# One product for the first 64 queries of a sliding-window attention block, with the low parts of the probabilities in the unused half of the rows

## The chip, the cores and the metric

The kernel runs on one core of one Trainium2 chip. The metric is the device time of one execution, in microseconds (us). A core has the engines TensorE (PE; weight loads are shown as PEld), VectorE (DVE), ScalarE (ACT), GpSimd (POOL) and SyncE (SP, which here only issues transfers), an SBUF of 128 partitions, and PSUM for the results of products.

## The reference

One transformer layer on 512 tokens of width 2048: RMS norm, sliding-window attention with a learned bias and sinks, a gate, an output projection, then a gated embedding and a final norm. Cut to what matters here (32 heads of 64 in 4 key-value heads; blocks of 128 queries):

```python
q, k, v, gate = jnp.split(h @ w_in, [...], axis=-1)
dist = qi + BLOCK - kj
band = (dist >= 0) & (dist < WINDOW)          # WINDOW = 128
scores = einsum('bnqhgd,bnjhd->bnhgqj', q, kb) * HEAD_DIM ** -0.5 + bias
scores = where(mask, scores, finfo.min)
m = maximum(scores.max(-1), sink)
e = exp(scores - m)
probs = e / (e.sum(-1) + exp(sink - m))
out = einsum('bnhgqj,bnjhd->bnqhgd', probs, vb)
y = (out * silu(gate)) @ w_out
```

A query sees its own key and the 127 before it. The first 64 queries therefore see at most 64 keys.

## The kernel before

All products keep float32 accuracy with operands that are split in two: a rounded high part (type fp32r) and a low part, the remainder. A weight product is three products, high by high, high by low and low by high (`mm3`, L123).

**Stages.** The first stage (loop over 16 slabs k, L199) computes keys, values and the first two chunks of queries while it loads x. The second (L850 to L915) runs everything else of the attention: the remaining query chunks and all gate chunks as a stream of products (`projections`, L829), and between them 64 attention blocks. The third and fourth are the output projection and the gated embedding, both as Strassen-like schemes whose combined weights are summed in DRAM during the second stage (`sum_weights`, L663): SP copies a block of weights (L666), and GpSimd adds another to the copy with an accumulating transfer (L668), which must wait for the copy to land. Copies and additions are spread over the blocks; eight copies are issued in the first one (`SUMS_EARLY`).

**An attention block.** Block i belongs to a quad of heads d = i // 8 and to 64 queries g = i % 8 (`UNITS` is 8, `TWOS` is 8). It runs through three generators in successive turns of the main loop, with the projection's products between their steps:
- `scores(i)` (L449): two products on TensorE into the one PSUM tile of the tag w; GpSimd puts the sink into a column and fills masked columns (L477, L480); VectorE adds the bias and takes the maximum (L485 to L494); ScalarE takes the exponentials with their sum (L498) and writes the normalised probabilities `pr` (L509).
- `turn(i)` (L511), two turns later: TensorE transposes pr (L518), so that keys lie on the partitions; ScalarE takes the high part `r[:, 0]` (L523), VectorE the low part `r[:, 1]` (L524). For g of 2 and more GpSimd cuts out a triangle, `own` (L534).
- `weigh(i)` (L546), one turn later: TensorE multiplies the values with r, high and then low part (L559, L560). The values V[t] hold, for each key-value head, 64 columns of high and 64 of low parts, so that one product gives both (L360); the two halves of the result are added on ScalarE and VectorE (L571, L573).

**Values.** At the end of the first stage VectorE scales the values of four token tiles and splits V[0] (L374 to L380, `split` at L362). The splits of V[1] to V[3] and the differences DV of neighbouring tiles are made in the first blocks (`first_chores`, L430); SP spreads the differences over partitions (L428).

**Order.** In the second stage the order on all engines is the order in which the program is written. Each engine's queue is taken in order, SP's too: a transfer that waits holds up all that SP issues after it. SP's order around the change is: the last weights of the first stage; the four transfers of the first bias (`load_bias(0)`, L851, which reads a table that GpSimd wrote to DRAM); the weight slabs of the projections (`Weights.load`, L99), each 128 x 1024 floats, in a pool of three; the first eight copies of the weight sums; a further slab; the differences DV. A slab is split by ScalarE and VectorE (`Weights._make`, L104), in order with the work of the attention blocks on these engines.

**Tiles.** Pools are stacked. `mid` holds the keys and values, then the attention's pool `attn`, which takes the room of the first stage's pool `start`. A tile whose room was used before waits for the old users.

Of the kernel before, what the change touches and what calls it, by code (L numbers as in the profile page):

```python
# [11 lines left out]
F32 = mybir.dt.float32  # L12
F32R = mybir.dt.float32r
# [7 lines left out]
P = 128  # L21
KC = D // P
NB = S // P
HEADS = 32
KVH = 4
HD = 64
# [3 lines left out]
HB = P // 2  # L30
# [8 lines left out]
MASKED = -3.0e38  # L39
# [16 lines left out]
def trunk_kernel(ctx: ExitStack, tc: tile.TileContext, a: dict):  # L56
    nc = tc.nc
# [18 lines left out]
    mid = ExitStack()  # L76
# [44 lines left out]
    W = Weights(ahead=2)  # L121
# [60 lines left out]
    kinds, g = [], 0  # L182
# [16 lines left out]
    for k in range(KC):  # L199
# [7 lines left out]
        both = start_pool.tile([P, 2, 768], F32R, tag="w0s", name=f"w0s{k}")  # L207
# [11 lines left out]
        h = room.tile([P, S], F32R, tag="ah", name=f"xh{k}")  # L219
        l = room.tile([P, S], F32R, tag="al", name=f"xl{k}")  # L220
# [36 lines left out]
        f, e = k == 0, k == KC - 1  # L257
# [26 lines left out]
        if 3 <= k < 3 + NB:  # L284
            t = k - 3
# [74 lines left out]
    V = [kvq.tile([P, KVH, 2, HD], F32R, name=f"V{t}") for t in range(NB)]  # L360
# [13 lines left out]
    for t in range(NB):  # L374
        nc.vector.tensor_scalar_mul(values[t], v_ps[t][:, :256], rstd1[:, t : t + 1])
        nc.vector.scalar_tensor_tensor(
            out=values[t], in0=v_ps[t][:, 256:], scalar=rstd1[:, t : t + 1], in1=values[t], op0=ALU.mult, op1=ALU.add
# [11 lines left out]
    for b in range(exact, BUCKETS):  # L389
        d = np.nonzero(bk == b)[0]  # L390
        if len(d):
            lo, n = P - 1 + int(d.min()), len(d)
# [4 lines left out]
    pre.close()  # L397
    banks_s.close()
    spsum = mid.enter_context(tc.tile_pool(name="psum_w", bufs=1, space=PSUM))
    apool = mid.enter_context(tc.tile_pool(name="attn", bufs=1, reuse_waits="tile"))  # L400


# [3 lines left out]

    U, T, PT, O, gates, biases = {}, {}, {}, {}, {}, {}

    DV = apool.tile([P, NB - 1, 2, KVH * 2 * HD], F32R, name="DV")
    apool.tile([P, 8], F32, name="pad2")  # L410
    diffs = {}

    def make_diff(n):
# [35 lines left out]
    def scores(i):  # L449

        d, g = divmod(i, UNITS)
        if g == 4 and d + 1 < TWOS:
            load_bias(d + 1)
        key = K[d // 2]

        s_ps = spsum.tile([P, 2, S], F32, tag="w", name=f"s{i}")  # L460
        number = [min(2 * g + u + 1, 5) * QB for u in range(2)]
        for u in range(2):
            first, n = max(2 * g + u - 4, 0) * QB, number[u]
            st = Q[d][:, 2 * g + u].rearrange("p h q -> p (h q)")
            nc.tensor.matmul(s_ps[:, u, : 2 * n], st, key[:, :, first : first + n], start=True, stop=True)  # L465
        W = KEYS + 2
        t = apool.tile([P, 2, W], F32, tag="t", name=f"t{i}", bufs=3)
        at = t[:, 0, 0:1]

        def two(of, stride, n):  # L470
            return bass.AP(tensor=at.tensor, offset=at.offset + of, ap=[at.ap[0], [stride, 2], [1, n]])

        late = QB if g >= 2 else 0
        seen = [t[:, 0, 0 : P + 1], t[:, 1, 1 + late : P + 2 + late] if late else t[:, 1, 0 : P + 1]]
        both = two(0, W + 1 + late if late else W, P + 1)
        pr = [t[:, u, 1 + late * u : 1 + late * u + P] for u in range(2)]
        nc.gpsimd.tensor_copy(two(0, W + W - 1 if late else W, 1), sinkb[:, d : d + 1].unsqueeze(1).to_broadcast([P, 2, 1]))  # L477
        for u, n in enumerate(number):
            if n < P:
                nc.gpsimd.memset(t[:, u, 1 + n : 1 + P], MASKED)  # L480
        yield
        bias = biases[d][:, ::-1]
        if g < 2:
            for u, n in enumerate(number):
                nc.vector.tensor_add(t[:, u, 1 : 1 + n], s_ps[:, u, :n], bias[:, KEYS - n :])  # L485
            for u, n in enumerate(number):
                nc.vector.tensor_add(t[:, u, 1 : 1 + n], s_ps[:, u, n : 2 * n], t[:, u, 1 : 1 + n])
        else:
            x = t[:, :, 1 : 1 + KEYS]
            nc.vector.tensor_add(x, s_ps[:, :, :KEYS], bias.unsqueeze(1).to_broadcast([P, 2, KEYS]))  # L490
            nc.vector.tensor_add(x, s_ps[:, :, KEYS : 2 * KEYS], x)
            nc.vector.tensor_max(two(1, W + P, QB), t[:, :, 1 : 1 + QB], t[:, :, 1 + P : 1 + KEYS])
        sm = apool.tile([P, 24], F32, tag="sm", name=f"sm{i}", bufs=4)
        nc.vector.tensor_reduce(sm[:, 0:2], both, axis=AX.X, op=ALU.max, negate=True)  # L494
        yield
        for u in range(2):
            su = seen[u]
            nc.scalar.activation(su, su, AF.Exp, bias=sm[:, u : u + 1], accum_out=sm[:, 2 + u : 3 + u])  # L498
        yield
        nc.vector.reciprocal(sm[:, 4:6], sm[:, 2:4])  # L500
        yield

        T[i] = apool.tile([P, 2, P], F32, tag="pr", name=f"pr{i}", bufs=3)
        for u in range(2):
            out, src = T[i][:, u], pr[u]
            if late and (g + u) % 2:
                out = out.rearrange("p (h k) -> p h k", h=2)[:, ::-1]
                src = src.rearrange("p (h k) -> p h k", h=2)
            nc.scalar.mul(out, src, sm[:, 4 + u : 5 + u])  # L509

    def turn(i):  # L511


        d, g = divmod(i, UNITS)
        pr = T.pop(i)
        pt = bank(f"pt{i}", "t")[:, :256]
        for u in range(2):
            nc.tensor.transpose(pt[:, u * P : (u + 1) * P], pr[:, u, :], ident)  # L518

        r = apool.tile([P, 2, 256], F32R, tag="r", name=f"r{i}", bufs=2)  # L520
        rh, rl = (r[:, l].rearrange("p (h u q) -> p u h q", h=4, u=2) for l in range(2))
        src = pt.rearrange("p (u h q) -> p u h q", u=2, h=4)
        nc.scalar.copy(rh, src)  # L523
        nc.vector.tensor_sub(rl, src, rh.bitcast(F32))  # L524
        yield
        own = None
        if g >= 2:
            own = apool.tile([P, 2, 256], F32R, tag="own", name=f"own{i}", bufs=2)
            rows = slice(0, P) if g % 2 else slice(0, HB)
            flat = lambda v: v[rows].rearrange("p l (u q) -> p (l u) q", q=HB)  # L530


            sign = -1 if g % 2 else 1
            nc.gpsimd.affine_select(  # L534
                out=flat(own), in_=flat(r).bitcast(F32), pattern=[[0, 8], [sign, HB]], compare_op=ALU.is_ge, fill=0.0,
                base=-HB - 1 if g % 2 else 0, channel_multiplier=-sign,
            )
        PT[i] = (r, own)
        yield
        if own is not None:  # L540
            here, there = slice(HB, P), slice(0, HB)
            if g % 2 == 0:
                here, there = there, here
            nc.scalar.copy(own[there, 0], own[here, 1].bitcast(F32))

    def weigh(i):  # L546

        d, g = divmod(i, UNITS)
        n, b = divmod(g, 2)
        kv = d // 2  # L550
        r, own = PT.pop(i)
        if g == 0:
            U[d] = apool.tile([P, 2, S], F32, tag="u", name=f"u{d}", bufs=3)
        if b == 0:
            O[d] = bank(f"o{i}", "o").rearrange("p (b u e q) -> p b u e q", b=2, u=2, e=2)
        ops = O[d]
        out = ops[:, b].rearrange("p u e q -> p (u e q)")
        first = V[0 if n == 0 else n - 1 + b][:, kv]
        for low in range(2):  # L559
            nc.tensor.matmul(out, first, r[:, low], start=low == 0, stop=own is None and low == 1)  # L560
        if own is not None:
            nc.tensor.matmul(
                out, DV[:, n - 1, b, kv * 2 * HD : (kv + 1) * 2 * HD], own[:, 0], start=False, stop=True
            )
        yield
        if b:
            dst = U[d][:, :, n * P : (n + 1) * P].rearrange("p u (b q) -> p b u q", b=2)
            lower, upper = slice(0, 64), slice(64, 128)
            tmp = [apool.tile([P, 2, 2, HB], F32, tag=f"tmp{e}", name=f"tmp{e}_{i}", bufs=1) for e in range(2)]
            for e, (o, x) in enumerate(((lower, upper), (upper, lower))):  # L570
                nc.scalar.copy(tmp[e][o], ops[x, :, :, e, :])  # L571
            for e, o in enumerate((lower, upper)):
                nc.vector.tensor_add(dst[o], ops[o, :, :, e, :], tmp[e][o])  # L573
        if g == UNITS - 1:
            for c in (2 * d, 2 * d + 1):
                weighed.add(c)
                if c in open_gates:
                    idle.append(partial_of(gate_value, c))
# [67 lines left out]
    for (nm, p), small in zip(SUMS, (7, 5, 6, 4, None, None)):  # L646
        for m in range(2 if small else 0):
            t = summed["small", small, m] = tc.dram_tile([P, WE], F32, name=f"small_{small}_{m}")
# [5 lines left out]
        for jj in range(2):  # L654
            for m in range(4):
                t = summed[nm, p, jj, m] = tc.dram_tile([P, WE], F32, name=f"{nm}_{p}_{jj}_{m}")
# [265 lines left out]
    late = pool("late", reuse_waits="tile")  # L922
# [350 lines left out]
    f = ple_forms.made[4]  # L1273
# [18 lines left out]
    two = gate(3, 1, ps, e)  # L1292
# [143 lines left out]
```

## Time and profile before

Times are of the kernel as a whole. The profiled execution is a run of its own; its span is the time between its first and last instruction.

| | us |
|---|---|
| runs | 794.17, 794.43, 794.76; median 794.43 |
| span of the profiled execution | 792.6 |
| TensorE busy | 782.8 (99% of the span) |
| VectorE busy | 600.1 (76%) |
| ScalarE busy | 507.5 (64%) |
| GpSimd busy | 123.8 (16%) |

How to read it: the share of busy time is of the whole span. The chain of waits follows the work that ended last back from the end, at each step to what released it. A view in order of time has one row per instruction or per run of equal ones: start, duration, engine, line, operation, output and input tile, sizes, count, and in brackets how long the engine sat idle before it and what ended that. Lines are those of the kernel before. Transfers are shown when they are issued ("SPq"); another view gives the time from issue to landing. q1 is SP's transfer queue and q0 GpSimd's; both are worked off by the same 16 transfer engines. Times run from the span's start.

### The profile page before, as it was taken

The page shows a single profiled execution, that of the slowest core. Times are in us where ns is not written, and L with a number is a line of the kernel's source. Part 1 is how long each engine was busy: PE and PEld are TensorE (multiplying, and loading weights), DVE is VectorE, ACT ScalarE, POOL GpSimd, SP SyncE. Part 2 cuts the span into 40 slices and gives each one's busy share as a digit, 9 for nine tenths or more (in the row PEclk, how much of TensorE's full clock was granted, in tenths as well). Part 3 has the DMA queues.
Part 4 walks back from the last instruction along what each step waited for, and adds up shares of the span by engine and source line. Part 5 has one row for each costly group of instructions (what it writes and reads, how often), then busy time and mean ns, then how long its engine had stood idle before and what let it go on. Part 6 is the DMA issues. An engine that isn't in the chain of part 4 may idle for free.

```text
span 792.6 us, 11069 instructions
## 1 busy us (share of the span) xinstructions
PE 782.8 (99%) x3746; PEld 655.7 (83%) x3746; DVE 600.1 (76%) x1043; ACT 507.5 (64%) x1066; POOL 123.8 (16%) x248
## 2 busy tenths in 40 slices
PE   9999999999999999999999999999999999999995
PEld 8888888888888888888888888888888888888885
DVE  4556697877878687877777899778866757988896
ACT  6742576666767586766666654466699656656765
POOL 0201413131212213122222200000000120210000
PEclk9999999999999999999999999999999999999998
DMA  8987999797989989898987498667864996787633
GB/s 337 300 215 259 211 272 302 213 277 205 280 226 263 236 246 253 233 249 233 242 230 183 137 366 326 209 209 227 282 240 142 345 204 197 159 229 217 180 107 106
DMA packets 45065, 185.22 MB, mean 234 GB/s; under 512 B 6656, under 2 KB 7680, under 8 KB 39888
## 3 DMA queue, kind: packets, MB, share of 16 engines
q1 hardware_dynamic: 36928, 143.30, 53.3%
q0 software_dynamic: 8080, 41.22, 27.1%
q8 instruction: 29, 0.48, 0.2%
q14 instruction: 28, 0.23, 0.1%
HBM read 177.63 MB, written 62.97 MB: 304 GB/s over the span
## 4 chain that ended last, share of the span: by engine, by line
PE 99%; DVE 0%; ACT 0%; ACTq 0%; issue 0%; DVEq 0%
PE gps L128 7%; PE gps L127 7%; PE gps L126 7%; PE qps L126 7%; PE qps L128 7%; PE qps L127 7%; PE g L128 6%; PE o L127 6%; PE g L126 6%; PE o L128 6%; PE o L126 5%; PE g L127 5%; PE s L465 2%; PE o L560 2%; PE vps L279 2%; PE pt L518 2%
## 5 line engine op out<-in xcount | busy, mean ns | idle before, releaser
L705 DVE TENSOR_TENSOR blo<-braw,bhi 128x1024 fp32r<-128x1024 f32 x102 | 124.3, 1221 | 41.6 <-ACT bhi L704 41.3
L704 ACT CAST bhi<-braw 128x1024 fp32r<-128x1024 f32 x102 | 107.3, 1052 | 73.6 <-PE o L128 24.9
L128 PE MATMUL gps<-xh,wlo 128*128 128x512 f32 x256 | 99.9, 390 | 0.0
L127 PE MATMUL gps<-xl,whi 128*128 128x512 f32 x256 | 99.8, 390 | 0.0
L126 PE MATMUL gps<-xh,whi 128*128 128x512 f32 x256 | 99.8, 390 | 0.0
L126 PE MATMUL qps<-xh,whi 128*128 128x512 f32 x224 | 87.7, 391 | 0.0
L128 PE MATMUL qps<-xh,wlo 128*128 128x512 f32 x224 | 87.5, 390 | 0.0
L127 PE MATMUL qps<-xl,whi 128*128 128x512 f32 x224 | 87.3, 390 | 0.0
L126 PE MATMUL g<-bhi,fhg 128*128 128x512 f32 x192 | 75.1, 391 | 0.0
L110 DVE TENSOR_TENSOR wlo<-wraw,whi 128x1024 fp32r<-128x1024 f32 x60 | 73.5, 1226 | 1.9 <-ACT whi L109 1.5
L126 PE MATMUL o<-bhi,fho 128*128 128x512 f32 x192 | 74.8, 390 | 0.0
L128 PE MATMUL g<-bhi,flg 128*128 128x512 f32 x192 | 74.8, 389 | 0.0
L128 PE MATMUL o<-bhi,flo 128*128 128x512 f32 x192 | 74.8, 389 | 0.0
L127 PE MATMUL g<-blo,fhg 128*128 128x512 f32 x192 | 74.7, 389 | 0.0
L127 PE MATMUL o<-blo,fho 128*128 128x512 f32 x192 | 74.7, 389 | 0.0
L534 POOL TENSOR_SCALAR_AFFINE_SELECT own<-r 64x512 fp32r<-64x512 f32 (+1 forms) x48 | 32.4, 675 | 249.0 <-DVE r L524 241.5
L524 DVE TENSOR_TENSOR r<-pt,r 128x256 fp32r<-128x256 f32 x64 | 27.1, 423 | 55.4 <-ACT r L523 54.6
L523 ACT CAST r<-pt 128x256 fp32r<-128x256 f32 x64 | 23.7, 371 | 70.6 <-PE pt L518 70.2
L109 ACT CAST whi<-wraw 128x1024 fp32r<-128x1024 f32 x60 | 62.3, 1040 | 4.6 <-issue 4.1
L128 PEld LDWEIGHTS gps<-xh,wlo 128*128 128x128 f32 x256 | 48.0, 188 | 10.1
L498 ACT ACTIVATE t<-t,sm 128x129 f32<-128x129 f32 x128 | 50.6, 397 | 8.5 <-DVE sm L494 7.0
L126 PEld LDWEIGHTS gps<-xh,whi 128*128 128x128 f32 x256 | 48.1, 188 | 9.0
(228 smaller groups left out, 1741.3 us busy)
## 6 DMA issues: line engine op xcount, KB each, us to landing
wraw<-in_w_gate_in SPq DMA_DIRECT2D x32, 512.0 KB, 7.1
w_out<-in_w_out POOLq DMA_DIRECT2D x32, 512.0 KB, 8.0
braw<-w_out SPq DMA_DIRECT2D x32, 512.0 KB, 4.8
wraw<-in_w_q SPq DMA_DIRECT2D x28, 512.0 KB, 5.2
braw<-in_ple_gate SPq DMA_DIRECT2D x24, 512.0 KB, 4.3
braw<-in_w_out SPq DMA_DIRECT2D x22, 512.0 KB, 4.3
xw<-in_first SPq DMA_DIRECT2D x14, 640.5 KB, 7.1
w_out<-in_w_out SPq DMA_DIRECT2D x16, 512.0 KB, 10.1
```

The lines of the kernel that those rows point to most:

```text
L109: nc.scalar.copy(hi, raw)
L110: nc.vector.tensor_sub(lo, raw, hi.bitcast(F32))
L126: nc.tensor.matmul(ps, sh, mh, start=first, stop=False, skip_group_check=more)
L127: nc.tensor.matmul(ps, sh, ml, start=False, stop=False, skip_group_check=more)
L128: nc.tensor.matmul(ps, sl, mh, start=False, stop=last, skip_group_check=more)
L279: nc.tensor.matmul(v_ps[t], h[:, c], both[:, :, 256:512], start=f, stop=e, skip_group_check=True)
L498: nc.scalar.activation(su, su, AF.Exp, bias=sm[:, u : u + 1], accum_out=sm[:, 2 + u : 3 + u])
L523: nc.scalar.copy(rh, src)
L524: nc.vector.tensor_sub(rl, src, rh.bitcast(F32))
L534: nc.gpsimd.affine_select(out=flat(own), in_=flat(r).bitcast(F32), pattern=[[0, 8], [sign, HB]], compare_op=ALU.is_ge, fill=0.0, base=-HB ...
L704: nc.scalar.copy(hi, raw)
L705: nc.vector.tensor_sub(lo, raw, hi.bitcast(F32))
```

## The change

For g = 0, the first 64 queries of each quad of heads, only 64 keys exist. The changed kernel writes the normalised probabilities of these 64 keys twice, side by side, so that after the transpose both halves of the partitions hold them. ScalarE takes the high part of all 128 rows into `r[:, 0]`, and VectorE overwrites the upper 64 rows with the low part. A new tile `twice` holds the first 64 rows of V[0] in both halves of its partitions; two transfers on SP's queue fill it, right after the pools of the attention are opened. One product of `twice` with `r[:, 0]` takes the place of the two products of V[0] with high and low part. The scores' tile is filled, reduced and exponentiated over 64 columns and the sink where it was 128 and the sink. DV, pr, r and own move with `twice` into a pool of their own, `operands`, ahead of `attn`; a padding tile of 8 floats goes.

```diff
+    operands = mid.enter_context(tc.tile_pool(name="operands", bufs=1, reuse_waits="tile"))
     apool = mid.enter_context(tc.tile_pool(name="attn", bufs=1, reuse_waits="tile"))
...
-    DV = apool.tile([P, NB - 1, 2, KVH * 2 * HD], F32R, name="DV")
-    apool.tile([P, 8], F32, name="pad2")
+    DV = operands.tile([P, NB - 1, 2, KVH * 2 * HD], F32R, name="DV")
+    twice = operands.tile([P, KVH * 2 * HD], F32R, name="twice")
+    for o in range(2):
+        src = V[0][:HB].rearrange("p h l d -> p (h l d)").bitcast(F32)
+        nc.sync.dma_start(twice[HB * o : HB * o + HB].bitcast(F32), src)
...
+        near = P if g else HB
+        if g == 0:
+            seen = [v[:, : near + 1] for v in seen]
+        both = two(0, W + 1 + late if late else W, near + 1)
+        pr = [t[:, u, 1 + late * u : 1 + late * u + near] for u in range(2)]
...
-            if n < P:
-                nc.gpsimd.memset(t[:, u, 1 + n : 1 + P], MASKED)
+            if n < near:
+                nc.gpsimd.memset(t[:, u, 1 + n : 1 + near], MASKED)
...
+            if g == 0:
+                out, src = out.rearrange("p (h k) -> p h k", h=2), src.unsqueeze(1).to_broadcast([P, 2, HB])
...
         nc.scalar.copy(rh, src)
-        nc.vector.tensor_sub(rl, src, rh.bitcast(F32))
+        if g == 0:
+            nc.vector.tensor_sub(rh[HB:], src[HB:], rh[HB:].bitcast(F32))
+        else:
+            nc.vector.tensor_sub(rl, src, rh.bitcast(F32))
...
-        for low in range(2):
+        if g == 0:
+            nc.tensor.matmul(out, twice[:, kv * 2 * HD : (kv + 1) * 2 * HD], r[:, 0], start=True, stop=True)
+        for low in range(2 if g else 0):
             nc.tensor.matmul(out, first, r[:, low], start=low == 0, stop=own is None and low == 1)
```

More of the change, by code (lines that the diff above doesn't have):

```diff
@@ L474, in scores @@
         seen = [t[:, 0, 0 : P + 1], t[:, 1, 1 + late : P + 2 + late] if late else t[:, 1, 0 : P + 1]]
-        both = two(0, W + 1 + late if late else W, P + 1)
-        pr = [t[:, u, 1 + late * u : 1 + late * u + P] for u in range(2)]
+        near = P if g else HB
[3 more added lines that the diff above has]
+        pr = [t[:, u, 1 + late * u : 1 + late * u + near] for u in range(2)]
         nc.gpsimd.tensor_copy(two(0, W + W - 1 if late else W, 1), sinkb[:, d : d + 1].unsqueeze(1).to_broadcast([P, 2, 1]))
         for u, n in enumerate(number):
-            if n < P:
-                nc.gpsimd.memset(t[:, u, 1 + n : 1 + P], MASKED)
+            if n < near:
+                nc.gpsimd.memset(t[:, u, 1 + n : 1 + near], MASKED)
         yield
@@ L501, in scores @@
         yield
-        T[i] = apool.tile([P, 2, P], F32, tag="pr", name=f"pr{i}", bufs=3)
+        T[i] = operands.tile([P, 2, P], F32, tag="pr", name=f"pr{i}", bufs=3)
         for u in range(2):
             out, src = T[i][:, u], pr[u]
+            if g == 0:
+                out, src = out.rearrange("p (h k) -> p h k", h=2), src.unsqueeze(1).to_broadcast([P, 2, HB])
             if late and (g + u) % 2:
@@ L518, in turn @@
             nc.tensor.transpose(pt[:, u * P : (u + 1) * P], pr[:, u, :], ident)
-        r = apool.tile([P, 2, 256], F32R, tag="r", name=f"r{i}", bufs=2)
+        r = operands.tile([P, 2, 256], F32R, tag="r", name=f"r{i}", bufs=2)
         rh, rl = (r[:, l].rearrange("p (h u q) -> p u h q", h=4, u=2) for l in range(2))
@@ L527, in turn @@
         if g >= 2:
-            own = apool.tile([P, 2, 256], F32R, tag="own", name=f"own{i}", bufs=2)
+            own = operands.tile([P, 2, 256], F32R, tag="own", name=f"own{i}", bufs=2)
             rows = slice(0, P) if g % 2 else slice(0, HB)
```

## The prediction

> **What bounds the kernel now.** I read the page first, for the busy shares and the chain that ended last.
>
> ```profile
> PE 782.8 (99%) x3746; PEld 655.7 (83%) x3746; DVE 600.1 (76%) x1043; ACT 507.5 (64%) x1066; POOL 123.8 (16%) x248
> PE 99%; DVE 0%; ACT 0%; ACTq 0%; issue 0%; DVEq 0%
> ```
>
> TensorE is busy 99% of the span and is itself the chain. So a product taken away is worth its own spacing, a microsecond by which TensorE has to wait is a microsecond of the kernel, and work on the other engines is free until TensorE waits for it. The change adds two transfers to SP's queue, so the second view is the order of time of that queue between the first stage (keys, values, first queries) and the attention, with VectorE's beside it. Columns: start, duration, engine, line, operation, count.
>
> ```profile
> 63.02 1.72 SPq L447 DMA_DIRECT2D bias<-tdram  x4
> 64.84 0.84 SPq L102 DMA_DIRECT2D wraw<-in_w_q  x2
> 65.73 1.23 SPq L666 DMA_DIRECT2D small<-in_w_out  x2
> 67.01 4.35 SPq L666 DMA_DIRECT2D w_out<-in_w_out  x6
> 81.28 0.35 SPq L102 DMA_DIRECT2D wraw<-in_w_gate_in  x1
> 89.12 2.42 SPq L428 DMA_DIRECT2D DV<-diffs  x4
> 91.59 0.58 SPq L102 DMA_DIRECT2D wraw<-in_w_gate_in  x1
> ...
> 79.16 0.41 DVE L365 TENSOR_TENSOR V<-values,V 128x256 fp32r<-128x256 f32 x1
> ```
>
> From 63.0 to 71.4 us SP issues the first bias, two weight slabs (call them W4 and W5, counting the loads of L102 from 0) and eight copies of 512 KB (c1 to c8) that begin the weight sums. W6 follows at 81.28, W7 at 91.59. The low half of V[0] is finished only at 79.16 + 0.41 = 79.57.
>
> **The change part by part.** *Removed.* One of two 256-column products in each of the eight g = 0 blocks. The spacing of such products, from a run of four near the end (first and last), and in place:
>
> ```profile
> 782.52 0.28 PE L127 MATMUL last<-low,fhg 128*128 128x256 f32 x1
> ...
> 782.88 0.28 PE L127 MATMUL e<-blo,pTh 128*128 128x256 f32 x1
> ...
> 97.42 0.48 PE L560 MATMUL o<-r,V 128*128 128x256 f32 x2
> 97.73 0.46 PE L465 MATMUL s<-k,q 128*128 128x320 f32 x2
> ```
>
> (782.88 - 782.52) / 3 = 0.12 us; in place (97.73 - 97.42) / 2 = 0.155. I take 0.14: 8 x 0.14 = 1.1 us gained (1.0 to 1.2). That is below 0.2% of the time, 1.6 us, which is about what a measurement of this kernel can tell from no change.
>
> *Shortened, at nothing.* Exponentials over 65 columns for 129, a shorter maximum, eight fill operations fewer on POOL, and a subtraction of the same width on half the partitions: all on engines at 76% and less. The new product waits for that subtraction as the second one did before. The moved tiles change no order on any engine in the built program.
>
> *Added.* Two transfers of 128 KB into `twice`, ahead of the first bias on SP's queue, and they wait for V[0]. SP issues in order, so everything behind them waits too: the bias, W4, W5, c1 to c8, W6. The DV transfers have the same shape, and four take 2.42 us, so two take 1.2: the bias goes out at 79.57 + 1.2 = 80.8 for 63.02, a shift of 17.8 us. It is priced by when each transfer lands. The rows are issues with their time to landing in us, from narrow windows: the fourth bias (issued 64.32), W4 (64.84), W5 (65.30), c1 (65.73), c8 (70.35), W6 (81.28), W7 (91.59), then POOL's accumulations a1 (81.80) and a5 (88.09).
>
> ```profile
> bias<-tdram SPq DMA_DIRECT2D x1, 20.0 KB, 2.0
> wraw<-in_w_q SPq DMA_DIRECT2D x1, 512.0 KB, 4.0
> wraw<-in_w_q SPq DMA_DIRECT2D x1, 512.0 KB, 5.0
> small<-in_w_out SPq DMA_DIRECT2D x1, 512.0 KB, 7.8
> w_out<-in_w_out SPq DMA_DIRECT2D x1, 512.0 KB, 13.4
> wraw<-in_w_gate_in SPq DMA_DIRECT2D x1, 512.0 KB, 4.3
> wraw<-in_w_gate_in SPq DMA_DIRECT2D x1, 512.0 KB, 12.0
> ...
> small<-in_w_out POOLq DMA_DIRECT2D x1, 512.0 KB, 7.1
> w_out<-in_w_out POOLq DMA_DIRECT2D x1, 512.0 KB, 12.3
> ```
>
> Bias: 66.3 becomes 84.1, while the second block's scores (TensorE at about 87) need the first's two additions (0.7 us) done: covered. W4: 68.8 becomes 86.6. ScalarE splits it at 81.98 now, and the first probabilities, which stand behind it on ScalarE, end at 86.85 + 0.70 = 87.55, that is 5.6 us later, for a transpose at 91.97:
>
> ```profile
> 81.98 1.05 ACT L109 CAST whi<-wraw 128x1024 fp32r<-128x1024 f32 x1 [4.08 <-issue]
> ...
> 86.85 0.70 ACT L509 ACTIVATE pr<-t,sm 128x128 f32<-128x128 f32 x2 [0.23 <-DVE sm L500]
> ...
> 91.97 0.38 PE L518 MATMUL pt<-ident,pr 128*128 128x128 f32 x2
> ```
>
> 86.6 + 5.6 = 92.2: some 0.2 us late, nearly covered. W6 is the costly one. If c1 to c8 only shift, c1 lands at 73.6 + 17.8 = 91.4 and c8 at 83.8 + 17.8 = 101.6. But POOL's a1 may start once c1 has landed, so the accumulations, which today run after the copies, now run among them. What that does is seen where POOL's queue (q0) and SP's (q1, the DV transfers) overlap today, from 94 to 97 us (packets, MB, share of the 16 engines; the third row is q0 from 83.0 to 84.2, its first packets there):
>
> ```profile
> q0 software_dynamic: 85, 0.57, 93.0%
> q1 hardware_dynamic: 84, 0.14, 14.2%
> ...
> q0 software_dynamic: 2, 0.02, 11.2%
> ```
>
> They take turns packet by packet, 85 to 84, and one of POOL's holds an engine 0.93 x 16 x 3 / 85 = 0.53 us by this row; alone, a1 to a5 land from 88.9 to 100.4, with the DV transfers among the last of them, so I take 0.6 for each of the four packets that an engine has of an accumulation (512 KB in packets of 0.57 MB / 85, 6.7 KB on the mean with small closing ones among them, over 16 engines). A copy is one packet on each engine, (101.6 - 91.4) / 7 = 1.46 us; a weight slab has 128 rows of 4 KB, eight on each engine, and W4 and W5 land 1.5 us apart, 0.18 a packet. Today a1's first packets run just before 84.2, about 2.3 us after its issue at 81.80; issued at about 91.4 it starts at 93.7. From there c8 lacks 7.9 us, 5.4 turns, each made longer by 0.6: 101.6 + 3.2 = 104.8. W6's eight packets then take 8 x (0.18 + 0.6) = 6.2: W6 lands at 111.0. Its bounds: 101.6 + 1.5 = 103.1 if q1 goes first, and 103.1 + 5 x 2.4 = 115.1 if all five accumulations do.
>
> Who waits for W6 is in ScalarE's order of time: the split of W6 and, behind it, pr of block 3; the split of W7 and pr of block 4; and TensorE's transposes of them.
>
> ```profile
> 99.29 1.05 ACT L109 CAST whi<-wraw 128x1024 fp32r<-128x1024 f32 x1
> ...
> 103.90 0.69 ACT L509 ACTIVATE pr<-t,sm 128x128 f32<-128x128 f32 x2 [0.30 <-DVE sm L500]
> ...
> 104.80 1.04 ACT L109 CAST whi<-wraw 128x1024 fp32r<-128x1024 f32 x1
> ...
> 109.14 0.69 ACT L509 ACTIVATE pr<-t,sm 128x128 f32<-128x128 f32 x2
> ...
> 108.35 0.27 PE L518 MATMUL pt<-ident,pr 128*128 128x128 f32 x1
> ...
> 114.00 0.27 PE L518 MATMUL pt<-ident,pr 128*128 128x128 f32 x1
> ```
>
> From split to pr's end it is 5.3 us (VectorE's low part, a query split and the reciprocal lie between), and the transpose comes at 108.35, so W6 may land until 108.35 - 5.3 - 0.2 = 102.8 without a wait. At 111.0 TensorE waits 8.2 us there (0.3 to 12.3). W7 is not an addition to it but a second check of the same delay: behind W6 stand the DV transfers (16 packets, 1.6 us alone) and W7 (1.5), with 20 - 5.4 - 8 = 6.6 accumulation packets left (4.0): 111.0 + 7.1 = 118.1. It may land until 114.00 - 5.0 - 0.2 = 108.8: 9.3 late in all. The later slabs come as far behind W7 as today, so TensorE, 9 us late itself, then meets them.
>
> A wait of 8 us has one more price. At the end of the kernel and at its start the trace shows what idleness does to TensorE's granted clock (columns of the windows: stretch and length, busy of PE, PEld, DVE, ACT, POOL, clock, DMA share, GB/s).
>
> ```profile
> 783.40:786.00 2.60, 0.24 (x3) 0.04 (x1) 2.31 (x10) 2.29 (x4) 0.00 (x0) 1.00 0.00 0
> 786.00:787.40 1.40, 0.00 (x0) 0.00 (x0) 1.26 (x5) 1.14 (x4) 0.00 (x0) 0.99 0.00 0
> 787.40:790.00 2.60, 0.00 (x0) 0.00 (x0) 0.33 (x1) 0.37 (x1) 0.00 (x0) 0.50 0.92 295
> ...
> 4.17 1.22 PE L265 MATMUL qps<-xh,w0s 128*128 128x256 f32 x4
> ...
> 5.61 0.70 PE L265 MATMUL qps<-xh,w0s 128*128 128x256 f32 x4
> ```
>
> The clock halves 787.4 - 783.6 = 3.8 us after the last product, and at the start four products of 256 columns take 1.22 us at 4.17 and 0.70 from 5.61 on, so TensorE has come to its full pace by about 5.6. So after an 8 us gap TensorE may run at half speed for up to some 5 us: 0 to 2.5 lost, I take 2. [...]
>
> *Sum.* Wait at block 3's transpose 8.2 + half clock 2.0 = 10.2, which covers W7's 9.3; less 1.1: +9.1 us. Against the profiled execution's span of 792.6 that is 801.7; what lies around the span, 794.43 - 792.6 = 1.8, is taken as unchanged: **803.5 us**.
>
> **The rivals.** (a) *Hidden after all, not slower.* W6 lands at 103.1 because SP's copies keep their 1.46 us beside the accumulations, 0.3 us late; then W7 is in time (103.1 + 1.6 + 1.5 = 106.2, under 108.8) and the products decide: 794.43 + 0.3 - 1.1 = 793.6. For it: W6 has 13.7 us to spare today (85.6 to 99.29). Against: the shift is 17.8, and the 85-to-84 row. It decides up to a landing at 103.9, where the wait eats the 1.1 gained. (b) *Partly hidden.* The accumulations start later or cost less among copies, W6 lands around 106: 3.2 us of wait, too short for the clock, and W7 around 113, 4 us late: 794.43 + 4.2 - 1.1 = 797.5. For it: 0.53 us per packet in the row, not 0.6. (c) *Turns by whole transfers.* A queue is served a whole transfer's packets before the other: a copy (1.46) per accumulation (2.4) from 93.7, so 5.4 x 2.4 = 13.0, of which there are only 12: c8 at 113.6, W6 at 115.1, 12.3 of wait plus 2: 794.43 + 14.3 - 1.1 = 807.6. Against: both kinds in the row have four packets per engine and transfer, so it doesn't exclude this, but equal counts over only 3 us speak for single turns. [...] (d) *A real gain*, above 1.6 us, would need TensorE to wait for softmax work today; the chain shows 99% TensorE.
>
> **How the numbers follow.** Forecast 0.66, (b) 0.13, (c) 0.08, (a) 0.10, (d) 0.03. The likeliest case alone, with the clock's 0 to 2.5 and W6 at 109 to 113, spans 800 to 806. Holding 8 in 10 means taking in (b) and (c): 796.5 to 808.0. Slower than 0.2%: 0.66 + 0.13 + 0.08 = 0.87; within it 0.10; faster 0.03.
>
> **What would show it.** In the changed profile: SP's bias transfers issued at 80 to 81 us; W6 landing at 109 to 113; ScalarE idle before its split for a DMA; one TensorE gap of about 8 us ahead of block 3's transpose, near 108 us, followed by lower granted clock; the eight lone products of the g = 0 blocks; and from some 130 us on the old rhythm of 5.65 us a block. Wrong would be: no TensorE gap, or gaps that recur in every pair, or W6 in before 103 us.

## The result, and the profile after

| | before | changed |
|---|---|---|
| median of the runs | 794.43 us (794.09 to 795.12) | 808.85 us (808.54 to 810.0) |
| span of the profiled execution | 792.6 us | 808.3 us |
| TensorE busy | 782.8 us (99%) | 787.1 us (97%) |

The change makes the kernel slower: ratio 1.0184, 95% interval 1.0173 to 1.0195, or 14.4 us between the medians. The prediction had 803.5 us and a range to 808.0. The profiled execution of the changed kernel took 810.0 us, 1.2 us above its median, so a sum over its trace should come out near 15.6.

The page of the changed kernel: its busy times, the chain that ended last, TensorE and its granted clock in 40 slices of 20 us, and the rows of the groups that show a new idle time.

```profile
PE 787.1 (97%) x3738; PEld 657.6 (81%) x3738; DVE 600.0 (74%) x1043; ACT 506.6 (63%) x1066; POOL 124.4 (15%) x240
...
PE   9999959999999999999999999999999999999995
...
PEclk9999989999999999999999999999999999999998
...
PE 91%; DMA 4%; DVE 2%; ACT 1%; SPq 1%; issue 0%; ACTq 0%; DVEq 0%
...
L109 ACT CAST whi<-wraw 128x1024 fp32r<-128x1024 f32 x60 | 62.3, 1041 | 25.1 <-DMA wraw<-in_w_gate_in 15.1
```

Eight products and eight fills are gone (3738 for 3746, 240 for 248), and yet TensorE is busy 4.3 us longer: part of its work ran at a lower clock. The chain now has 4% of transfers and 1% of SP's queue. TensorE's idle time is in the sixth slice, 101 to 121 us, with the lower clock. The waits of TensorE (engine and line, what it waited for: us in total, times, longest) show that it is two gaps there, one forecast and one not:

```profile
PE gps L126 <- DVE q L321: 8.2, 1, 8.2
PE o L576 <- ACT own L556: 3.0, 2, 2.8
...
PE pt L527 <- ACT pr L518: 0.4, 1, 0.4
```

The row left out, 0.9 us at the very start, is the only one that the kernel before has too (0.8). SP's queue in order of time, at the place where the prediction read it:

```profile
80.12 1.17 SPq L414 DMA_DIRECT2D twice<-V  x2
81.39 1.93 SPq L451 DMA_DIRECT2D bias<-tdram  x4
83.35 0.90 SPq L102 DMA_DIRECT2D wraw<-in_w_q  x2
84.30 1.20 SPq L680 DMA_DIRECT2D small<-in_w_out  x2
85.54 4.06 SPq L680 DMA_DIRECT2D w_out<-in_w_out  x6
90.71 0.34 SPq L102 DMA_DIRECT2D wraw<-in_w_gate_in  x1
...
101.04 0.33 SPq L102 DMA_DIRECT2D wraw<-in_w_gate_in  x1
```

The bias goes out at 81.39 instead of 63.02, and everything behind it moves with it; W6 goes out at 90.71 and W7 at 101.04, both 9.4 us later than before. Their issue is not what costs. These are the times from issue to landing of W4 (issued 83.35), c8 (89.11), W6 and W7, each from a narrow window of the changed kernel:

```profile
wraw<-in_w_q SPq DMA_DIRECT2D x1, 512.0 KB, 4.5
...
w_out<-in_w_out SPq DMA_DIRECT2D x1, 512.0 KB, 16.6
...
wraw<-in_w_gate_in SPq DMA_DIRECT2D x1, 512.0 KB, 21.1
...
wraw<-in_w_gate_in SPq DMA_DIRECT2D x1, 512.0 KB, 19.7
```

So c8 lands at 105.7, W6 at 111.8 and W7 at 120.7, the slabs 26.2 and 17.1 us later than before (85.6 and 103.6). ScalarE in order of time shows who stands behind the two slabs in the changed kernel:

```profile
111.80 1.04 ACT L109 CAST whi<-wraw 128x1024 fp32r<-128x1024 f32 x1 [10.22 <-DMA wraw<-in_w_gate_in]
...
120.79 1.04 ACT L109 CAST whi<-wraw 128x1024 fp32r<-128x1024 f32 x1 [3.39 <-DMA wraw<-in_w_gate_in]
121.86 0.74 ACT L585 COPY tmp<-o 64x256 f32<-64x256 f32 x2
122.51 0.40 ACT L556 CAST own<-own 64x256 fp32r<-64x256 f32 x1
```

VectorE's part between W6's split and the products:

```profile
112.88 1.23 DVE L110 TENSOR_TENSOR wlo<-wraw,whi 128x1024 fp32r<-128x1024 f32 x1 [10.40 <-ACT whi L109]
114.12 1.39 DVE L321 TENSOR_TENSOR q<-qps,q 64x512 fp32r<-64x512 f32 x2
```

TensorE in order of time, the last product ahead of the first gap and the first behind each:

```profile
107.09 0.39 PE L128 MATMUL qps<-xh,wlo 128*128 128x512 f32 x1
115.66 0.76 PE L126 MATMUL gps<-xh,whi 128*128 128x512 f32 x1 [8.18 <-DVE q L321]
...
122.96 0.58 PE L576 MATMUL o<-own,DV 128*128 128x256 f32 x1 [2.82 <-ACT own L556]
```

W6 lands at 111.8; its high part (1.04), its low part (1.23) and the query split behind that (1.39), which empties the PSUM bank, follow at once, and 3.9 us after the landing the first product of the next chunk of gates starts, 8.18 us late. W7 lands at 120.7. Its split stands ahead of the copy of `own` on ScalarE, and the product with `own` starts 2.82 us late. What the clock did to the work between, in windows (stretch and length, busy of PE, PEld, DVE, ACT, POOL, granted clock, DMA share, GB/s):

```profile
107.50:112.60 5.10, 0.00 (x0) 0.00 (x0) 0.00 (x0) 0.80 (x1) 0.00 (x0) 1.00 1.04 234
112.60:119.40 6.80, 3.75 (x9) 3.00 (x10) 5.40 (x11) 2.27 (x9) 0.81 (x2) 0.50 1.01 255
119.40:122.80 3.40, 0.74 (x6) 0.44 (x4) 0.93 (x1) 1.97 (x4) 0.00 (x0) 1.00 0.53 126
122.80:126.20 3.40, 3.24 (x9) 2.75 (x10) 3.31 (x9) 2.23 (x9) 0.71 (x2) 0.50 1.05 284
```

There are two stretches at half clock, one after each gap. Work of 3.75 and of 3.24 us at 0.50 lost half of that, 1.9 and 1.6 us (the product with `own` at 122.96 took 0.58 us there; one of the same size takes 0.28 at 135.85, where the clock is 1.00). The transfer engines, by contrast, are full throughout the first gap: the slabs were late because there was that much to move ahead of them. What had been lost stands earlier in the two pages, in the row of the transfer engines' busy share over 40 slices, first before, then changed:

```profile
DMA  8987999797989989898987498667864996787633
DMA  9870999989799999989896588767782997796633
```

In the fourth slice, about 60 to 80 us, they are at seven tenths before (259 GB/s) and next to idle in the changed kernel (26 GB/s). While SP waits for V[0] hardly anything is fetched, and what was not fetched then stands ahead of W6 and W7.

### The profile page after: what moved, and what is told of

Read it like the earlier page. It is cut to its first block, busy times and chain, and to the rows that moved or that the text cites. A ratio compares the mean times of both kernels' runs of the same rounds, so it can differ in the third digit from the quotient of the medians.

```text
span 808.3 us, 11051 instructions
## 1 busy us (share of the span) xinstructions
PE 787.1 (97%) x3738; PEld 657.6 (81%) x3738; DVE 600.0 (74%) x1043; ACT 506.6 (63%) x1066; POOL 124.4 (15%) x240
## 4 chain that ended last, share of the span: by engine, by line
PE 91%; DMA 4%; DVE 2%; ACT 1%; SPq 1%; issue 0%; ACTq 0%; DVEq 0%
PE gps L126 7%; PE gps L127 7%; PE gps L128 7%; PE qps L126 6%; PE qps L128 6%; PE qps L127 6%; PE o L127 5%; PE o L128 5%; PE o L126 5%; PE g L127 5%; PE g L126 5%; PE g L128 5%; DMA wraw<-in_w_gate_in 2%; PE s L469 2%; PE vps L279 2%; DMA w_out<-in_w_out 2%
## 5 line engine op out<-in xcount | busy, mean ns | idle before, releaser
L110 DVE TENSOR_TENSOR wlo<-wraw,whi 128x1024 fp32r<-128x1024 f32 x60 | 73.5, 1227 | 21.2 <-ACT whi L109 21.1
L127 PEld LDWEIGHTS gps<-xl,whi 128*128 128x128 f32 x256 | 48.8, 191 | 9.1
L505 ACT ACTIVATE t<-t,sm 128x129 f32<-128x129 f32 (+1 forms) x128 | 49.7, 390 | 7.8 <-DVE sm L501 6.3
```

The source lines that it names most:

```text
L110: nc.vector.tensor_sub(lo, raw, hi.bitcast(F32))
L127: nc.tensor.matmul(ps, sh, ml, start=False, stop=False, skip_group_check=more)
```

## The experiments

The theory after this result: the two transfers hold SP's queue until V[0] is split, so the eight early copies, GpSimd's accumulations and the weight slabs meet in one heap; the loss is the wait for W6 and a second one at W7, each with its half clock, and the new arithmetic is a small gain. The rivals: the arithmetic itself costs, or the moved tiles; the late bias costs; the copies alone cost, without the accumulations.

**The transfers without the arithmetic, and the arithmetic without the early transfers.** The first kernel is the one before with only the transfers added; the second is the changed kernel with the transfers behind the eight copies.

```diff
     DV = apool.tile([P, NB - 1, 2, KVH * 2 * HD], F32R, name="DV")
-    apool.tile([P, 8], F32, name="pad2")
+    twice = apool.tile([P, KVH * 2 * HD], F32R, name="twice")
+    for o in range(2):
+        src = V[0][:HB].rearrange("p h l d -> p (h l d)").bitcast(F32)
+        nc.sync.dma_start(twice[HB * o : HB * o + HB].bitcast(F32), src)
```

> The kernel before with only the two transfers added in the place where the change puts them (and the padding tile left out for room); nothing reads the tile twice, and the two products stay. Queue theory: the loss is there without any of the new arithmetic, and without its gain: 808.85 + 0.6 to 1.1, so 809 to 811, with the gap of about 8 us before the products of W6 and one of about 3 us before those of own. Rival (arithmetic or tiles): 794 to 796.

```diff
-    for o in range(2):
+
+    def load_twice():
         src = V[0][:HB].rearrange("p h l d -> p (h l d)").bitcast(F32)
-        nc.sync.dma_start(twice[HB * o : HB * o + HB].bitcast(F32), src)
+        for o in range(2):
+            nc.sync.dma_start(twice[HB * o : HB * o + HB].bitcast(F32), src)
...
             for n in sums_in(i):
                 sum_weights(n)
+        if i == 0:
+            load_twice()
```

> The changed kernel with the two transfers into twice moved behind the eight early copies on SP's queue, nothing else. Queue theory (the whole loss is the queue that stands behind the two transfers while they wait for V[0]): the bias is issued at 63 us again and c1 to c8 from 66 on, the transfers at 79.6 to 80.8, W6 still at about 81.3; no wait of TensorE, no low clock, and only the saved products count: 793.3 to 793.9 (the blocks after the stall gained 0.08 us each in the changed kernel's trace, 0.6 in all; 1.1 by the prediction). Rival (the new product itself, the wait for its operands or the moved tiles cost): still 800 or more.

The transfers alone took 811.61 us, ratio 1.021 (1.0196 to 1.0224), 0.6 us above the expected range, with the same two waits of TensorE, both somewhat longer:

```profile
PE gps L126 <- DVE q L321: 8.8, 1, 8.8
PE o L565 <- ACT own L547: 4.0, 2, 2.3
```

The changed kernel with late transfers took 793.41 us, ratio 0.999 (0.9981 to 0.9999). TensorE's only wait is the 0.8 us at the start again, and SP's queue has its old order, with W4, W5 and the eight copies right behind the bias:

```profile
59.86 1.72 SPq L454 DMA_DIRECT2D bias<-tdram  x4
...
80.00 1.14 SPq L416 DMA_DIRECT2D twice<-V  x2
81.63 0.34 SPq L102 DMA_DIRECT2D wraw<-in_w_gate_in  x1
```

The two transfers still wait for V[0] until 80.0, but nothing urgent stands behind them now. All of the loss is their place in the queue; arithmetic and moved tiles are not to blame. This version is faster than both kernels, than the one before by 0.1%, only just clear of the noise.

**What the two transfers cost where they stand in nobody's way.** The kernel before, with the transfers at that late place.

```diff
-    apool.tile([P, 8], F32, name="pad2")
+    twice = apool.tile([P, KVH * 2 * HD], F32R, name="twice")
+
+    def load_twice():
...
+        if i == 0:
+            load_twice()
```

> The kernel before with the two transfers added behind the eight early copies (and without the padding tile); the two products stay and nothing reads twice. Queue theory: they cost nothing there, 794.2 to 795.0; and the step to the same place with the new product, 793.41, is then the product's. Rival (the transfers cost or the tiles gain): 793.4, or 796 and more.

Measured: 794.29 us against 794.36, ratio 1.0000 (0.9991 to 1.0008). They cost nothing there. Beside the run before, 793.41, that leaves 0.9 us for the new arithmetic: 0.11 per product taken away (the interval of that run alone allows 0.1 to 1.5 us). The traces are sharper than the times: from the first product with r to the scores behind it are 0.31 us before (97.42 to 97.73) and 0.20 in the late version (97.78 to 97.98), and in each of the eight g = 0 blocks, there and in the changed kernel, this stretch is 0.12 us shorter, 0.9 in all.

**The bias ahead of the transfers.** The four transfers of the first bias keep their time; the slabs and copies stay behind the transfers into `twice`.

```diff
...
     load_bias(0)
+    load_twice()
     W.apart = True
```

> The changed kernel with the first bias ahead of the two transfers, everything behind them as in the changed kernel. Queue theory by way of W6 and W7: the bias counts for nothing, the loss stays: 808 to 810 (W4 goes out 1.8 us earlier, and so do the copies: at best 807). Rival (the late bias holds up the first softmax and so the rest): back to 794 to 796.

Measured: 808.15 us, ratio 1.0166 (1.015 to 1.0181), waits of 7.3 and 2.6 us at the same two places. The late bias is not the cause.

**The changed kernel without the first five accumulations.**

```diff
-        elif i % 2 == 1 and 0 <= i // 2 - 3 < len(adds):
+        elif i % 2 == 1 and 5 <= i // 2 - 3 < len(adds):
             nc.gpsimd.dma_start(*adds[i // 2 - 3], accum_op=ALU.add, max_dma_last_dim=8192)
```

> The changed kernel without GpSimd's first five accumulating transfers (a1 to a5; that part of the weight sums is left out, everything else is done). If the accumulations' turns make W6 and W7 late: c1 to c8 land from 90.6 at 1.46 us each, c8 at 101, W6 at about 103 and W7 at about 106, in time for both waits: no wait but the 0.4 us at block 0's transpose, 793.5 to 795.5. If the copies alone suffice: gaps remain, 800 or more.

Measured: 798.37 us, ratio 1.0052 (1.0039 to 1.0066). The waits of TensorE, then ScalarE's split of W6:

```profile
PE o L576 <- ACT own L556: 2.1, 2, 1.1
PE gps L126 <- DVE q L321: 1.6, 1, 1.6
```

```profile
104.76 1.05 ACT L109 CAST whi<-wraw 128x1024 fp32r<-128x1024 f32 x1 [3.69 <-DMA wraw<-in_w_gate_in]
```

Some 10 of the 14 us go with the five accumulations: W6 is there at 104.8 instead of 111.8. But the expectation was missed by 3 us. The shift alone, without any accumulation, is already too much, by 1.6 us of wait for W6 and 2.1 at the products with `own`: c8 lands at 101.2, as expected, but W6 only 3.5 us behind it, where some 2 were put. The clock stays at full behind these waits, 1.00 from 105 to 143 us.

**The copies ahead of the transfers, the slabs behind.**

```diff
...
     proj = projections()
+    for n in range(0, SUMS_EARLY, 2):
+        sum_weights(n)
+    load_twice()
     load_bias(0)
...
         if i == 0:
-            return range(0, SUMS_EARLY, 2)
+            return range(0)
```

> The changed kernel with the eight early copies issued ahead of the two transfers; the transfers, the first bias, W4 and W5 stay in the order of the changed kernel, so they are as late as there. If copies and accumulations in front of W6 and W7 make the loss: W6 lands before 90 us, at most some tenths of a us of wait from W4 at block 0's transpose, 793.3 to 795. If the late bias, W4 and W5 make it: no better than 805.

Measured: 801.45 us, ratio 1.0088 (1.0074 to 1.0102): between what the theories had. W6, expected before 90 us, landed at 99.3. TensorE's longest wait lies elsewhere, and W4, issued at 82.95, took 10.1 us to land:

```profile
PE pt L530 <- ACT pr L521: 4.9, 1, 4.9
```

```profile
wraw<-in_w_q SPq DMA_DIRECT2D x1, 512.0 KB, 10.1
```

With the copies long landed, GpSimd's accumulations go out at 81.9, beside the slabs and no longer beside the copies. Now W4 is late (93.1; the transposes of the first probabilities stand behind its split). It is the same cause at another slab: loaded beside the accumulations, it takes 2.5 times its 4.0 us of before.

**The second wait, taken away where it showed.** The split of W7 is put behind the attention work of its turn on ScalarE, so that the copy of `own` does not wait for it.

```diff
             if n == 0:
                 first_chores(i, 1)
-                some(W.todo)
+                if i != 4:
+                    some(W.todo)
...
             elif n == 5:
                 next(softmax, None)
+                if i == 4:
+                    some(W.todo)
```

> The changed kernel with one step moved: in block 4's turn of the loop the split of W7 stands behind that turn's attention work on ScalarE and VectorE (the copies out of o, the copy within own, the exponentials), not ahead of it. If the second wait of the changed kernel is own's copy standing behind W7's split, as its trace reads: the first gap of 8.2 us stays, the wait of 2.8 us of the product with own goes, and with it part of the half clock: 803.5 to 806. If TensorE would wait for W7 itself as long: 808 to 809.5. (W8's load moves behind the last DV transfers, which may cost 1 to 2 us later.)

Measured: 811.58 us, ratio 1.0215 (1.02 to 1.0231), against expectation. The wait for `own` behind W7 is gone, but the next one is there. TensorE and ScalarE in order of time:

```profile
129.22 0.58 PE L576 MATMUL o<-own,DV 128*128 128x256 f32 x1 [4.39 <-ACT own L556]
```

```profile
117.30 0.40 ACT L556 CAST own<-own 64x256 fp32r<-64x256 f32 x1
...
126.63 1.04 ACT L109 CAST whi<-wraw 128x1024 fp32r<-128x1024 f32 x1 [5.12 <-DMA wraw<-in_w_q]
```

`own` of W7's turn is copied at 117.30, ahead of W7's split, and the product with it no longer waits. So the place of the second wait was read rightly. But TensorE then runs on into W8, whose load had moved with the split, behind four DV transfers. To take that side effect out, one more run keeps each load at its place and moves the splits of both W7 and W8:

```diff
-                some(W.todo)
+                if i in (4, 5):
+                    W.load(len(W.raw) + 1)
+                else:
+                    some(W.todo)
...
                 next(softmax, None)
+                if i in (4, 5):
+                    some(W.todo)
```

> The changed kernel with the splits of W7 and of W8 both moved behind their turn's attention work on ScalarE, while the load of the next slab stays at its place in SP's order (in the run before, W8's load had moved with W7's split, behind four DV transfers, and W8's split then held the product with own by 4.39 us). Theory (the second loss is the product with own behind the split of a late slab, and nothing else): the first gap of 8.2 to 8.4 us ahead of chunk 3's first product stays, both waits for own vanish, only one stretch of half clock is left; 8.3 + 1.7 + 0.5 + 0.7 - 0.6 gives about 10.5 over before, 804 to 806 us. Rival (TensorE only meets the next late slab somewhere else, as in the run before): the sum of the gaps stays at 11 us or more and the time at 808 to 812 us. Rival (the two waits overlap as predicted, so that the second costs nothing of its own): no change from the changed kernel, 808 to 809 us.

Measured: 812.19 us, ratio 1.0227 (1.0213 to 1.0241). The first wait stays at 8.3 us; of the second, the row of the waits, then TensorE and ScalarE in order of time:

```profile
PE o L576 <- ACT own L556: 4.5, 1, 4.5
```

```profile
135.82 0.58 PE L576 MATMUL o<-own,DV 128*128 128x256 f32 x1 [4.48 <-ACT own L556]
```

```profile
132.27 1.04 ACT L109 CAST whi<-wraw 128x1024 fp32r<-128x1024 f32 x1 [5.19 <-DMA wraw<-in_w_q]
```

The theory as put there falls, and its first rival holds, with the time 0.2 us above its range: both waits behind W7 and W8 are gone, and TensorE meets W9 instead, 4.5 us long. The comparison with the changed kernel says why nothing was won. There the product with `own` of this same block starts without a wait:

```profile
135.85 0.28 PE L576 MATMUL o<-own,DV 128*128 128x256 f32 x1
```

135.82 against 135.85: TensorE stands at the same place at the same time, whichever late slab it has waited for (in this trace it had even been 1.1 us ahead at block 0's transpose, 91.90 for 92.98), and the later gap then costs a stretch of half clock of its own (0.55 on the mean from 133.6 to 137.0 us, 0.50 to 140.4). The slabs stay late for some 30 us, up to W9, and the wait can be moved along them but not taken away by the order of the splits. (That W9 lands later here, 132.3 against 130.7, may be due to an accumulation that GpSimd issues 3 us earlier in this run, 122.88 for 126.09; that was not tried by itself.)

## Why the prediction was right in kind and short in size

| step | predicted | measured in the changed kernel |
|---|---|---|
| bias issued | 80.8 | 81.4 |
| wait behind W4 | 0.2 | 0.4 |
| c8 lands | 104.8 | 105.7 |
| W6 lands | 111.0 | 111.8 |
| wait behind W6 | 8.2 | 8.2 |
| half clock after it | 2.0 | 1.9 |
| W7 lands | 118.1 | 120.7 |
| waits for `own`, behind W7 and once 0.2 later | "covered", 0 | 3.0, and 1.6 of half clock |
| products | -1.1 | -0.9 |
| sum | +9.1 | +14.2 (medians: +14.4) |

*The queue and the slab: right, the landing of c8 partly by luck.* Turns packet by packet, as the prediction read them from the 85-to-84 row, gave W6's landing to 0.8 us: behind c8 W6 took 111.8 - 105.7 = 6.1 us where 6.2 were forecast. In these us (105.7 to 110.8) the two queues moved, in packets, MB and share of the engines:

```profile
q0 software_dynamic: 126, 0.78, 77.7%
q1 hardware_dynamic: 127, 0.43, 25.4%
```

Rival (c), turns by whole transfers, had c8 at 113.6 and W6 at 115.1, and falls. The counts are equal again, 126 to 127; which packet followed which on one engine was not shown.

The landing of c8, 105.7 for 104.8, hides two errors. The accumulations' first packets move at 95.95 us and not at 93.7; until then the trace has packets of SP's queue alone. And without accumulations c8 lands at 101.2 (the run that leaves them out). So 5.3 us were left to it, 3.6 turns and not 5.4, and they cost 105.7 - 101.2 = 4.5 us, 1.2 a turn and not 0.6. From 96 to 104.7 the queues moved 115 and 102 packets. Of SP's 102, 47 are closing packets of 4 bytes, 35 are packets of copies, of 32 KB, and 20 are of W6, of 4 KB. Why a turn cost 1.2 us was not shown.

Rivals (a) and (b) fall with the landing too, and (a) twice over: without any accumulation W6 still came at 104.8, not 103.1, and the kernel lost 4 us.

*The place of the first gap: half right.* It lies in front of the first product of the next chunk of gates, and block 3's transpose, which the prediction named, comes only after nine more products. That product started at 106.30 before and needs W6 3.9 us earlier, so by 102.4, where the prediction had 102.8. W6 at 111.8 was 9.4 us late for that. But TensorE itself came to the gap 1.0 us later than before (its last product started at 107.09, for 106.08), half of which was there by 6.9 us, ahead of anything changed. That gives some 8.4, and 8.2 as the view counts it, from the end of the product before: the size was right partly by luck.

*The half clock: right for the gap that was priced.* 1.9 us against 2.0. The row has the clock at 1.00 until 112.6, 5.1 us after the last product, and not the 3.8 that the prediction read at the end of the kernel before. Why it fell later here was not shown.

*The step that failed:* "Wait at block 3's transpose 8.2 + half clock 2.0 = 10.2, which covers W7's 9.3". Two things were wrong in it. First, the limit of W7, "It may land until 114.00 - 5.0 - 0.2 = 108.8", was taken from pr of block 4 and its transpose. The first to wait is another, as rows of before show that were not quoted there: on ScalarE, behind W7's split at 104.80,

```profile
105.87 0.74 ACT L571 COPY tmp<-o 64x256 f32<-64x256 f32 x2
106.52 0.40 ACT L544 CAST own<-own 64x256 fp32r<-64x256 f32 x1
```

and on TensorE

```profile
108.80 0.28 PE L562 MATMUL o<-own,DV 128*128 128x256 f32 x1
```

From the split's start to the end of `own`'s copy it is 106.92 - 104.80 = 2.1 us, for a product at 108.80: W7 may land until 106.7, 2.1 us sooner than put. Second, W7 came at 120.7 and not 118.1: 9.0 us behind W6 (their splits start at 111.80 and 120.79), with 7.1 forecast. 2.1 and 2.6 together turn W7's 9.3 us of lateness into 14.0, and TensorE had lost 11.3 by then: 122.96 - 2.82 = 120.14, where before it was at 108.80. That leaves 2.7, the wait of 2.82 that the trace shows, to which a second stretch of half clock adds its 1.6.

Which term of the 7.1 was too small, the trace's packets tell. W6's last packet ends at 110.8; of W7's 128 packets of 4 KB the first moves at 115.7 and the last ends at 119.8. So the accumulations and DV transfers ahead of W7 took 4.9 us, where 4.0 + 1.6 were put, and W7 itself took 4.1, where the prediction put 1.5. The accumulations had no part in that: from 116.5 to 119.7 the trace has 1 packet of theirs, and of SP's queue

```profile
q1 hardware_dynamic: 370, 0.80, 102.0%
```

From 115.7 to 119.8 some 270 packets of 2 KB, the size of the DV transfers' alone, moved beside W7's. The four DV transfers ahead of W7 have 256, of which 165 were gone: most of the 270 belong to those issued behind W7. So the 1.5, from two slabs that followed each other without such company, did not hold. In the kernel before W7's packets took as long, 98.6 to 102.6, but TensorE did not wait for them there.

The sentence "The later slabs come as far behind W7 as today" held in the changed kernel: W8 and W9 landed 5.7 and 9.9 us behind W7 (126.5 and 130.7), for 5.5 and 10.5 before. That TensorE then meets them was so because it had lost 14 us and not 9 by then; in the last two runs, in which it did not wait for W7, it waited for W8 or W9.

*The sum.* 8.2 + 3.0 + 0.4 of waits, 1.9 + 1.6 of half clock, less 0.9 for the products: 14.2 us, beside 14.4 between the medians. The products gained 0.12 us each, the 0.12 of the prediction's first row and not its 0.14. The profiled execution is 15.7 longer, 1.5 us more. Set beside the one before product by product, 0.5 of these are there by 6.9 us, ahead of anything changed (four products of the first stage take 1.05 us from 5.67 on, for 0.70 from 5.61), and 0.3 come at about 490 us in the output projection, where the kernel before with late transfers loses 0.6 too; the rest lies at the edges of the waits.

## What to carry to other kernels

A small transfer that waits for a late result must not be issued, on a queue that is taken in order, ahead of transfers that others need earlier: two transfers with 1.2 us of issue cost 14 us here, as the transfer engines had next to nothing to do while SP waited (26 GB/s) and too much afterwards, and the same two transfers behind the eight copies cost nothing. When a shift makes several loads late, check for each of them every consumer that stands behind it in its engine's order, and add the lateness slab by slab until one is back in time; here a wait of 2.8 us saved at W7 was paid at the next late load, 4.4 us at W8 and, with that saved too, 4.5 at W9. And price a late load by what it now runs beside, the transfers issued behind it included, not by its duration in the old place (W4 took 10.1 us beside the accumulations, for 4.0 before).

## What the runs showed of the hardware

The accumulating transfers were the surprise in size. A 512 KB slab that lands 4 to 5 us after its issue beside plain transfers took 10.1 us beside accumulations (W4 with the copies first) and 21.1 in the heap of the changed kernel (W6), where copies were queued ahead of it as well; leaving out five accumulations of 512 KB gave back 10.5 us of the kernel's time (808.85 to 798.37).

The clock was dearer for short gaps than the prediction had it. Two more windows of the changed kernel, beside those above:

```profile
105.80:109.20 3.40, 1.68 (x8) 1.06 (x6) 0.00 (x0) 0.00 (x0) 0.00 (x0) 1.00 1.08 246
112.60:116.00 3.40, 0.34 (x1) 0.38 (x2) 3.06 (x5) 1.28 (x6) 0.00 (x0) 0.50 0.98 240
```

The stretch at half clock from 112.6 to 119.4 us followed the gap of 8.2 us: the clock was still 1.00 from 105.8 to 109.2, with 1.68 us of work, and until 112.6, with none. The stretch from 122.8 to 126.2 followed a gap of only 2.82 us, with 0.74 us of work from 119.4 to 122.8, where rival (b) of the prediction had held a wait of 3.2 us to be too short. The gaps of 1.6 and 1.1 us in the run without accumulations left the clock at 1.00 from 105 to 143 us. At what gap the clock falls, and whether its length alone decides, was not shown; no run was made to try it.
